# Four tiles of a PEER layer dense: another choice of tiles, and all routing ahead of the dense part

## The chip, the core and the metric

The kernel runs on one core of a Trainium2 chip. The time is device microseconds of one execution; the comparison goes by the median of several. Engines are named as the profile names them: PE (matrix products, with its weight loads as PEld), DVE (vector), ACT (scalar, activation functions), POOL (which issues the gathers of table rows) and SP (which issues all other DMAs). Each engine works through its own instructions in program order and waits where an operand isn't there.

## What is computed

One layer of a decoder trunk, for a prompt of 1024 tokens (tiles 0 to 7 of 128) and a sample group of 32 tokens (the "sample tile", `NT` in the code). Mixers first, then a projection with layer norm, then a PEER layer: each token scores 8 heads of 2 x 128 keys, picks 16 of 128 twice, 16 of the 256 sums, and so 128 experts of 16384; each expert has a row in `peer_u` and one in `peer_v`.

```python
x = layer_norm(ALPHA * x + g1 * mix(x * (1 + sc1) + sh1))
q = einsum('nd,de->ne', h, w_pq); s = einsum('nhpd,hpkd->nhpk', q, peer_keys)
s1, i1 = top_k(s[:, :, 0], 16); s2, i2 = top_k(s[:, :, 1], 16)
top_s, pos = top_k(s1[..., :, None] + s2[..., None, :], 16); idx = i1 * 128 + i2 (at pos)
act  = gelu(einsum('nd,nhkd->nhk', h, peer_u[idx]))
out  = einsum('nhk,nhkd->nd', softmax(top_s) * act, peer_v[idx])
x = layer_norm(ALPHA * x + g2 * out)
```

All inputs and outputs are float32.

## The kernel before

The PEER layer is done in two ways. For the tiles in `GATHERED` POOL gathers the rows that were picked: one gather brings 128 rows of 1024 floats (0.524 MB), one expert for each of 128 tokens. DVE multiplies a row of `peer_u` with the token and sums (L1300, 128 gathers a tile). Then, token by token, the 128 rows of `peer_v` are multiplied with their coefficients on PE (L1357, four instructions' worth for two gathers; a gather of this table is called an item). The sample tile takes 32 + 32 gathers. For the four tiles in `DENSE` the whole tables are streamed through PE: scores of 512 tokens with 128 blocks of 128 experts (`psd`, L1071, 24 matmuls of 512 columns each in three float16 products), GELU (L1161), a product with the gate matrix `G` (L1163), a split into two float16 parts (L1168, L1169), and the second product (`po`, L1178, 256 x 12 matmuls), which is added up in SBUF (L1187). 32 of the 128 score blocks (`PRE`) are done early, in `g_pre`, and parked in DRAM.

`G` comes from `g_weights`: for each dense token a one-hot matrix of the first index and one of the second, scaled by the gate, built by DVE (L1046 to L1049) and, for the last parts of `NL` of 16 tokens, by ACT (L1051); PE multiplies them (L1058), ACT copies PSUM to SBUF in two halves of 64 columns (L1061), and SP stores 32 tokens at a time to `G_d` (L1065).

Before either way, a tile is mixed (`g_mix`: projection with `w_o`, layer norm, transposes) and routed (`g_route`: 16 loads of `w_pq` for each group of tiles, L880, and the top 16 of each list on DVE, L900 to L904; `g_choice` and `g_select`: the second choice). Groups are in `FRONT` ([0, 1], [2, 3], [4, 5], [6]) and `BACK` ([7, NT]).

The order of instructions comes from generators that `run` steps by planned time: each yields estimates for PE, DVE and DMA, `PHASES` scales them by generator and phase, `AHEAD` gives priorities, and `wait` holds a generator until a name is in `ready`. `g_main` holds the dense part back until the gate matrices, the routing of `FRONT` and the early scores are planned; then it opens it (`late`), while `BACK` is mixed and routed beside the first dense steps. `g_gather` plans gathers at all times: rows of the first table of the next tile beside items of the second table of the one before. Both use one ring of six buffers of a row (`rows`, `NROW`). The result of gathered tiles is finished in `finish_tile` or, after the routing, in `g_finish`; dense tiles in `end`.

## Time and profile before

| | us |
|---|---|
| median of 3 runs (3184.49 to 3195.64) | 3193.88 |
| the profiled execution | 3195.18 |
| its span, first to last instruction | 3193.5 |
| mean granted clock of PE, share of full speed | 0.914 |
| PE busy / DVE busy | 2726.1 / 2205.3 |
| DMA moved | 979.03 MB |

The page cuts the span in 40 slices and gives each engine's busy share as a digit; PEclk is the granted clock of PE in tenths, DMA the mean busy share of the 16 DMA engines. A table by stretch gives the busy time of each engine between two times, the number of instructions in brackets, and, last, granted clock, DMA share and GB/s. An engine that is busy all the time bounds its stretch; one that is not may wait for another, and the idle time before its instructions names what ended the wait.

### The profile page before, as it was taken

What the parts mean: (1) busy time and instruction counts of PE and PEld (TensorE: products, weight loads), DVE (VectorE), ACT (ScalarE), POOL (GpSimd) and SP (SyncE); (2) the same over time, 40 slices, a digit from 0 to 9 for tenths busy, and PEclk for the clock granted to TensorE, in tenths of its full rate; (3) what the DMA queues carried; (4) which work ended last, traced back from release to release, by engine and by line L of the source; (5) the groups of instructions that cost most, each with busy time, mean ns of one, the idle gap of its engine ahead of it and who ended that gap; (6) DMA issues with size and microseconds to landing.
All of it is one profiled execution on the core that took longest, in us unless ns stands there. A gap on an engine that the chain in (4) does not pass through costs nothing.

```text
span 3193.5 us, 45027 instructions
## 1 busy us (share of the span) xinstructions
PE 2726.1 (85%) x16366; PEld 1405.0 (44%) x16366; DVE 2205.3 (69%) x5764; ACT 952.3 (30%) x1654; POOL 1312.7 (41%) x1096
## 2 busy tenths in 40 slices
PE   5888995387978699885566999999999999999996
PEld 3447953244546376433322663434444443333331
DVE  2443898867689789767747678848777765655547
ACT  3323234112102145446611223322332322322220
POOL 0000265645444444444434203444555554445443
PEclk7988997688979799997687999999999999999997
DMA  8754798899898899899898647999999999999986
GB/s 294 238 183 146 268 345 291 292 316 320 309 340 311 323 338 347 305 330 359 314 326 313 224 166 244 353 334 336 362 344 361 356 344 328 325 355 342 352 319 212
DMA packets 376498, 979.03 MB, mean 307 GB/s; under 512 B 37477, under 2 KB 116452, under 8 KB 372172
## 3 DMA queue, kind: packets, MB, share of 16 engines
q0 software_dynamic: 156672, 570.49, 49.5%
q1 hardware_dynamic: 219604, 405.67, 36.4%
q8 instruction: 128, 2.10, 0.3%
q14 instruction: 94, 0.77, 0.1%
HBM read 907.07 MB, written 69.02 MB: 306 GB/s over the span
## 4 chain that ended last, share of the span: by engine, by line
PE 49%; DMA 14%; issue 6%; DVE 5%; POOL 3%; ACT 2%; SPq 0%; POOLq 0%; DVEq 0%; ACTq 0%
PE po L1178 16%; PE psd L1071 16%; PE acc L1357 7%; DMA row<-in_peer_v,iT 7%; PE pqr L880 4%; DMA row<-in_peer_u,ii 4%; POOL row L1273 3%; PE py L809 2%; DVE row L1300 1%; DMA G_d<-gs 1%; ACT gs L1061 1%; PE pgm L1058 1%; DMA wo<-in_w_o 1%; PE pvp L279 1%; PE ps L890 1%
## 5 line engine op out<-in xcount | busy, mean ns | idle before, releaser
L1273 POOL DMA_INDIRECT row<-in_peer_u,ii x544 | 666.4, 1225 | 1035.4 <-DVE ii L1296 315.3
L1273 POOL DMA_INDIRECT row<-in_peer_v,iT x544 | 643.0, 1182 | 786.0 <-PE acc L1357 372.9
L1300 DVE SCALAR_TENSOR_TENSOR row<-row,x2u 128x1024 f32<-128x1024 f32 x544 | 660.2, 1217 | 320.7 <-DMA row<-in_peer_u,ii 304.0
L1071 PE MATMUL psd<-xd,us 128*128 128x512 f16 x3072 | 713.6, 383 | 21.4 <-ACT us L1088 14.2
L1178 PE MATMUL po<-vs,coef 128*128 128x512 f16 x3072 | 701.4, 380 | 1.0 <-DVE coef L1169 0.5
L1071 PEld LDWEIGHTS <-us 128*128 128x128 f16 x3072 | 294.6, 99 | 432.1 <-issue 86.7
L1178 PEld LDWEIGHTS <-coef 128*128 128x128 f16 x3072 | 291.6, 98 | 431.8 <-issue 95.4
L1357 PE MATMUL acc<-row,cexp 128*32 128x512 f32 x2176 | 332.6, 654 | 144.7 <-DMA row<-in_peer_v,iT 141.0
L880 PE MATMUL pqr<-x2T,wpq 128*128 128x128 f32 (+1 forms) x2304 | 283.8, 282 | 0.7 <-DVE ns_s L707 0.7
L880 PEld LDWEIGHTS pqr<-x2T,wpq 128*128 128x128 f32 x2304 | 275.6, 198 | 9.9 <-DVE CA L933 1.5
L1161 ACT ACTIVATE act<-psd,scale 128x512 f32<-128x512 f32 x96 | 65.8, 685 | 535.1 <-PE psd L1071 535.0
L1187 DVE SCALAR_TENSOR_TENSOR acc<-po,scale,acc 128x512 f32<-128x512 f32 x248 | 182.8, 744 | 44.7 <-PE po L1178 44.0
L1142 DVE SCALAR_TENSOR_TENSOR vs<-v,vs 128x1024 f16<-128x1024 f32 x128 | 155.9, 1219 | 55.6 <-ACT vs L1141 55.4
L1163 DVE SCALAR_TENSOR_TENSOR act<-act,scale,g 128x512 f32<-128x512 f32 x128 | 95.6, 748 | 140.8 <-ACT act L1161 138.0
L1141 ACT ACTIVATE vs<-v 128x1024 f16<-128x1024 f32 x128 | 134.1, 1054 | 186.0 <-PE po L1178 122.7
L809 PE MATMUL py<-wo,Y 128*128 128x512 f32 (+1 forms) x288 | 141.9, 638 | 32.8 <-DMA wo<-in_w_o 24.0
L1357 PEld LDWEIGHTS acc<-row,cexp 128*32 128x32 f32 x2176 | 48.1, 111 | 269.2 <-DMA row<-in_peer_v,iT 163.4
L1058 PE MATMUL pgm<-ab 128*128 128x128 f16 x1024 | 98.9, 251 | 64.5 <-DVE ab L1048 30.1
L1061 ACT ACTIVATE gs<-pgm 128x256 f32<-128x256 f32 x256 | 125.9, 641 | 49.8 <-PE pgm L1058 33.0
L279 PEld LDWEIGHTS <-w 128*128 128x128 f16 x2160 | 124.2, 100 | 23.7 <-issue 20.6
L1168 ACT ACTIVATE coef<-act 128x512 f16<-128x512 f32 x128 | 80.1, 626 | 153.7 <-DVE act L1163 153.3
L1125 DVE SCALAR_TENSOR_TENSOR us<-u,us 128x1024 f16<-128x1024 f32 x96 | 117.0, 1220 | 11.6 <-ACT us L1124 11.4
(345 smaller groups left out, 2874.2 us busy)
## 6 DMA issues: line engine op xcount, KB each, us to landing
v<-in_peer_v SPq DMA_DIRECT2D x128, 512.0 KB
u<-in_peer_uT SPq DMA_DIRECT2D x96, 512.0 KB
wpq<-in_w_pq SPq DMA_DIRECT2D x80, 512.0 KB
G_d<-gs SPq DMA_DIRECT2D x32, 1024.0 KB
g<-G_d SPq DMA_DIRECT2D x32, 1024.0 KB
wada<-in_w_ada SPq DMA_DIRECT2D x48, 512.0 KB
wf<-in_w_in SPq DMA_DIRECT2D x44, 512.0 KB
wo<-in_w_o SPq DMA_DIRECT2D x40, 512.0 KB
```

The source lines that it names most:

```text
L279: mm(out, lhsT=x if cs is None else y, rhs=y if cs is None else x, start=(i + k == 0), stop=(i == len(ps) - 1 and k == KD - 1))
L809: mm(py[t, e][:ns[t]], lhsT=Y_[t][:, k + j, :ns[t]], rhs=w[:, j, :], start=(k + j == 0), stop=(k + j == KD - 1))
L880: mm(pq[:, i, :ns[t]], lhsT=w[:, k, :], rhs=X2[t][:, k, :ns[t]], start=(k == 0), stop=(k == KD - 1))
L1061: S.activation(gs[e][:, :, t0:t0 + 4].rearrange("p c t -> p t c"), pg[:, :, 64 * e:64 * e + 64], AF.Copy)
L1071: mm(ps, lhsT=us[a][:, k, :], rhs=xd[:, :, b, k, :], start=(m == 0), stop=(m == 23))
L1141: S.activation(vs[:, 0], v, AF.Copy, scale=SV)
L1142: V.scalar_tensor_tensor(out=vs[:, 1], in0=v, scalar=SV, in1=vs[:, 0], op0=ALU.mult, op1=ALU.subtract)
L1178: mm(po, lhsT=d[:, a, i * P:(i + 1) * P], rhs=vs[:, b, c % 2, :], start=(m == 0), stop=(m == 3 * GROUP - 1))
L1187: V.scalar_tensor_tensor(out=a, in0=po, scalar=scale[:, 3:4], in1=a, op0=ALU.mult, op1=ALU.add)
L1273: nc.gpsimd.indirect_dma_start(out=s[:], out_offset=None, in_=A[table], in_offset=bass.IndirectOffsetOnAxis(ap=idx, axis=0))
L1300: V.scalar_tensor_tensor(out=s, in0=s, scalar=1.0, in1=x2, op0=ALU.mult, op1=ALU.mult, accum_out=sv[:, k:k + 1])
L1357: return mm(pv[e][g:g + 32, :], lhsT=l, rhs=s[:, e * 512:e * 512 + 512], start=(j == 0), stop=(j == nj - 1), skip_group_check=True)
```

## The change

- Tiles 3 to 6 are dense instead of 2 to 5; gathered are 0, 1, 2, 7 and the sample tile instead of 0, 1, 6, 7 and the sample tile.
- The groups of mixing and routing become [0, 1], [2, 3], [4, 5], [6, 7, NT], all ahead of the dense part. One PSUM tile takes the scores of up to two tiles and the sample tile, with one copy for all; some sample tiles move into other rings of buffers.
- The dense part waits for one thing more, `ample`: 96 items of the second gathered tile must be planned.
- Items of the third and later gathered tiles have a ring of six rows of their own (`rows2`). To make room, the table `delta` shrinks from 32 x 32 to 8 x 64, a constant of ones is a broadcast, and the x1 rows of the end take over buffers of the dense part.
- `g_gates` gets 5000 of priority and a factor of 0.2 instead of 0.7; its copies take all 128 columns at once, into one buffer that is stored in four parts; `NL` is 3 instead of 6.

```diff
-AHEAD = {"g_mixed": 1000, "g_routed": 1000, "g_even": 1000, "g_odd": 1000}
+AHEAD = {"g_mixed": 1000, "g_routed": 1000, "g_even": 1000, "g_odd": 1000, "g_gates": 5000}
...
-    ("build", {"g_gates": 0.7, "g_even": 0.5, "g_odd": 0.5, "g_mixed": 0.5, "g_routed": 0.5, "g_gather": 0.7}),
-    ("late", {"g_gather": 0.8}),
+    ("build", {"g_gates": 0.2, "g_even": 0.5, "g_odd": 0.5, "g_mixed": 0.5, "g_routed": 0.5, "g_gather": 0.7}),
+    ("dense", {"g_gather": 0.8}),
...
+NROW2 = 6
+AMPLE = 96
...
-GATHERED = (0, 1, 6, 7, NT)
-DENSE = (2, 3, 4, 5)
+GATHERED = (0, 1, 2, 7, NT)
+DENSE = (3, 4, 5, 6)
...
-FRONT = [0, 1], [2, 3], [4, 5], [6]
-BACK = [7, NT],
+GROUPS = [0, 1], [2, 3], [4, 5], [6, 7, NT]
...
-NL = 6
+NL = 3
...
             if b * BB % TB == 0:
-                gs = [sc.tile("gs", [P, 64, TB], F32, 2) for _ in range(2)]
+                gs = sc.tile("gs", [P, P, TB], F32)
...
-                for e in range(2):
-                    S.activation(gs[e][:, :, t0:t0 + 4].rearrange("p c t -> p t c"), pg[:, :, 64 * e:64 * e + 64], AF.Copy)
-                yield 0.6, 1.1, 0.4 * MB
+                S.activation(gs[:, :, t0:t0 + 4].rearrange("p c t -> p t c"), pg, AF.Copy)
+                yield 0.6, 1.1, 0
             if (b + 1) * BB % TB == 0:
-                for e in range(2):
-                    nc.sync.dma_start(G_d[i * (P // TB) + b * BB // TB, :, 64 * e:64 * e + 64, :], gs[e])
+                for e in range(4):
+                    c = slice(32 * e, 32 * e + 32)
+                    nc.sync.dma_start(G_d[i * (P // TB) + b * BB // TB, :, c, :], gs[:, c, :])
...
-                E[i] = cur["fin"].tile(f"e{i}", (P, D))
+                E[i] = sc.tile(f"e{i}", (P, D), F32, 2, "u" if i < 2 else "us")
...
-            if j > len(ops) - 60 and j % 3 == 0:
+            if j >= len(ops) - 8:
                 next(more, None)
...
-    def gather(table, idx):
-        s = cur["rows"].tile("row", (P, D), F32, NROW)
+    def gather(table, idx, own=False):
+        s = cur["rows2" if own else "rows"].tile("row", (P, D), F32, NROW2 if own else NROW)
...
-                    hold[q % 2] = gather("peer_v", iT[:, tok:tok + 1]), hold["c"][:, j % 2, q, :]
+                    hold[q % 2] = gather("peer_v", iT[:, tok:tok + 1], t not in GATHERED[:2]), hold["c"][:, j % 2, q, :]
...
         yield from wait("pre")
+        yield from wait("ample")
         for t in (NT - 1, NT):
             yield from wait(("y", t, 0))
         flush(0)
         cur["build"].close()
         cur["front"].close()
+        ready.add("dense")
         cur["dense"] = Scope("dense")
-        cur["fin"] = Scope("fin")
-        cur["front"] = Scope("late")
-        ready.add("late")
...
-        while "last" not in ready:
-            yield next(dense)
-        flush(0)
-        cur["front"].close()
-        cur["fin"].close()
+        cur["rows2"] = Scope("rows2", "right")
...
+                if done[0] == GATHERED[1] and iv == AMPLE:
+                    ready.add("ample")
```

SP where the dense part starts, before: `G_d<-gs` is the store of the gate matrix, `g<-G_d` its load, `u` a block of the first table, `Y`, `wo` and `keys` belong to the mixing and routing of the last group.

```order
L1065 DMA G_d<-gs 128x2048 x14
L1109 DMA g_13558<-G_d 128x16x128
L1109 DMA g_13607<-G_d 128x16x128
L1117 DMA u<-in_peer_uT 128x1024
L740 DMA g_15345<-ada_d 128x512
L1450 DMA x1f<-x_d 128x512
L800 DMA Y<-ycat_d 128x1024
L800 DMA Y<-ycat_d 128x8x32
L806 DMA wo<-in_w_o 128x2x512 x2
L871 DMA keys<-in_keysT 128x256 x2
```

The same place after: `sd_d<-so` parks the last early scores, the five `r_` rows are the parameters of the finish.

```order
L1090 DMA sd_d<-so 128x512 x3
L1391 DMA r_g_15397<-ada_d 128x1024
L1391 DMA r_ln_g<-in_ln_g 128x1024
L1391 DMA r_ln_b<-in_ln_b 128x1024
L1391 DMA r_ln_g<-in_ln_g 128x1024
L1391 DMA r_ln_b<-in_ln_b 128x1024
L1105 DMA g_15411<-G_d 128x16x128
L1113 DMA u<-in_peer_uT 128x1024 x2
L1131 DMA v<-in_peer_v 128x2x512 x2
L1105 DMA g_15460<-G_d 128x16x128
```

The loads of mixing and routing are gone from between the dense loads, the parameter rows stand there now, and no store of the gate matrix stands directly ahead.

POOL at the end of the program, before: gathers of the first table (`peer_u`) and of the second (`peer_v`).

```order
L1273 DMA row<-in_peer_u,ii 128x1024
L1273 DMA row<-in_peer_v,iT 128x1024 x3
L1273 DMA row<-in_peer_u,ii 128x1024
L1273 DMA row<-in_peer_v,iT 128x1024 x3
L1273 DMA row<-in_peer_u,ii 128x1024
L1273 DMA row<-in_peer_v,iT 128x1024 x71
```

And after:

```order
L1270 DMA row<-in_peer_u,ii 128x1024
L1270 DMA row<-in_peer_v,iT 128x1024
L1270 DMA row<-in_peer_u,ii 128x1024
L1270 DMA row<-in_peer_v,iT 128x1024 x2
L1270 DMA row<-in_peer_u,ii 128x1024
L1270 DMA row<-in_peer_v,iT 128x1024 x128
```

The first table's rows end 128 items before the end instead of 71.

DVE at the very end, before: `row<-pfold` is the sum of the sample tile's items, the last thing that was gathered.

```order
L786 SCALAR_TENSOR_TENSOR row<-row,mv,r_ln_b 128x1024
L1420 TENSOR_TENSOR row<-pfold,g2s 32x512 x2
L1425 TENSOR_TENSOR row<-row,x1f 32x1024
L781 BN_STATS st<-row 32x6 x2
L782 BN_AGGR mv<-st 32x2
L354 TENSOR_SCALAR ve<-mv 32x1
L785 SCALAR_TENSOR_TENSOR row<-row,mv,r_ln_g 32x1024
```

And after, where `acc` is the sum of a dense tile:

```order
L361 TENSOR_TENSOR mv<-vy,vy_25416 128x1
L360 TENSOR_SCALAR vy_25472<-vy_25472 128x1
L786 SCALAR_TENSOR_TENSOR acc_15409<-acc_15409,mv,r_ln_b 128x1024
L361 TENSOR_TENSOR mv<-vy,vy_25472 128x1
L786 SCALAR_TENSOR_TENSOR acc_15410<-acc_15410,mv,r_ln_b 128x1024
```

The program ended with the sample tile's gathered sum, and ends with two dense tiles now.

## Rows read from the trace of the kernel before

**Rows 1.** The page: span, DMA totals, one costly group (busy, mean ns of one).

```profile
span 3193.5 us, 45027 instructions
...
DMA packets 376498, 979.03 MB, mean 307 GB/s; under 512 B 37477, under 2 KB 116452, under 8 KB 372172
...
L1300 DVE SCALAR_TENSOR_TENSOR row<-row,x2u 128x1024 f32<-128x1024 f32 x544 | 660.2, 1217 | 320.7 <-DMA row<-in_peer_u,ii 304.0
```

**Rows 2.** Busy time by stretch: PE, PEld, DVE, ACT, POOL; clock, DMA share, GB/s.

```profile
0.00:350.00 350.00, 275.21 (x2186) 180.10 (x2187) 138.46 (x534) 110.71 (x209) 3.31 (x8) 0.88 0.62 208
350.00:1000.00 650.00, 498.93 (x3437) 325.67 (x3437) 529.65 (x1794) 148.89 (x282) 343.82 (x285) 0.84 0.91 322
1000.00:1210.00 210.00, 168.07 (x1174) 112.03 (x1173) 171.73 (x702) 58.96 (x124) 93.52 (x75) 0.89 0.89 317
1210.00:1300.00 90.00, 88.69 (x670) 57.02 (x671) 79.84 (x386) 47.72 (x96) 37.46 (x25) 1.00 0.88 331
1300.00:1602.00 302.00, 202.95 (x1410) 111.01 (x1402) 218.84 (x339) 172.41 (x391) 140.13 (x108) 0.82 0.91 333
1602.00:2000.00 398.00, 341.17 (x1739) 172.27 (x1739) 274.51 (x824) 94.82 (x155) 115.18 (x96) 0.92 0.75 254
...
2250.00:2600.00 350.00, 348.29 (x1708) 144.33 (x1707) 269.24 (x386) 103.81 (x129) 192.77 (x152) 1.00 0.98 355
...
2000.00:3150.00 1150.00, 1137.23 (x5709) 445.33 (x5707) 764.69 (x1093) 318.19 (x400) 568.53 (x490) 1.00 0.95 340
```

**Rows 3.** PE: the chain; L1071, L1178, L1357 in 2000:3150; a gather in 2250:2600.

```profile
1904.42 5.18 PE psd L1071 x24
...
2000.00:3150.00 1150.00, 422.83 (x1848) 176.17 (x1848) 1.00 0.95 340
2000.00:3150.00 1150.00, 584.37 (x2567) 243.34 (x2567) 1.00 0.95 340
2000.00:3150.00 1150.00, 176.10 (x1288) 25.77 (x1286) 1.00 0.95 340
...
L1273 POOL DMA_INDIRECT row<-in_peer_u,ii x89 | 110.1, 1237 | 64.8 <-DVE row L1300 35.7 <-issue 18.9 <-PE acc L1357 5.6
```

**Rows 4.** In 1602:2000: PE on L880, on L809; DVE on tiles TV, WK.

```profile
1602.00:2000.00 398.00, 61.20 (x512) 0.92 0.75 254
1602.00:2000.00 398.00, 33.81 (x64) 0.92 0.75 254
1602.00:2000.00 398.00, 41.97 (x284) 0.92 0.75 254
1602.00:2000.00 398.00, 18.04 (x40) 0.92 0.75 254
```

**Rows 5.** Groups in 1300:1602: busy us, mean ns, idle before and its releasers.

```profile
L1061 ACT ACTIVATE gs<-pgm 128x256 f32<-128x256 f32 x202 | 96.8, 642 | 44.1 <-PE pgm L1058 32.0 <-DMA G_d<-gs 11.9
L1273 POOL DMA_INDIRECT row<-in_peer_u,ii x62 | 83.1, 1341 | 86.1 <-DVE row L1300 39.6 <-PE acc L1357 33.8 <-issue 8.8
L1051 ACT ACTIVATE ab<-ab,fl 128x128 f16<-128x128 f16 x144 | 44.4, 392 | 40.4 <-DVE ab L1048 40.4
L1049 DVE TENSOR_TENSOR ab<-ab,fx 128x1280 f16<-128x1280 f16 x24 | 19.6, 820 | 0.1
```

**Rows 6.** The timeline at the first GELU of the dense part.

```profile
1602.13 0.69 ACT L1161 ACTIVATE act<-psd,scale 128x512 f32<-128x512 f32 x1 [3.55 <-PE psd L1071]
```

**Rows 7.** The timeline at the end of the dense part.

```profile
3142.71 3.41 PE L1178 MATMUL po<-vs,coef 128*128 128x512 f16 x15
...
3153.17 12.51 SPq L1204 DMA_DIRECT2D out_y_p<-acc  x4
```

**Rows 8.** DMA issues: count, KB each, median us to landing.

```profile
u<-in_peer_uT SPq DMA_DIRECT2D x96, 512.0 KB
...
g<-G_d SPq DMA_DIRECT2D x32, 1024.0 KB
...
row<-in_peer_u,ii POOLq DMA_INDIRECT x544, 7.5
```

More of the change, by code (lines that the diff above doesn't have):

```diff
@@ L112, in run @@
         now = 0.0
-        late = False
+        dense = False
         while parts:
-            if "late" in ready and not late:
-                late = True
+            if "dense" in ready and not dense:
+                dense = True
                 now = max(busy)
@@ L287, in load_consts @@
             C[nm] = load(nm, A[nm])
-        ones = C["ones"] = work("ones4", [4, P])
-        V.memset(ones, 1.0)
         o1 = C["ones1"] = work("ones1", [P, 1])
         V.memset(o1, 1.0)
+        C["ones"] = o1[0:4].to_broadcast([4, P])
         V.memset(Cst, 0.0)
@@ L798, in g_mix @@
             if t > 0:
-                Y_[t] = slab("Y", (P, KD, P))
+                Y_[t] = half("Y", (P, KD, NS)) if t == NT else slab("Y", (P, KD, P))
                 nc.sync.dma_start(Y_[t][:, :, :ns[t]], ycat_d[t, :, :, :ns[t]])
@@ L813, in g_mix @@
                 if t not in z:
-                    z[t] = slab("z")
+                    z[t] = (xslab if t == NT else slab)("z")
                 if t == ts[0] or t == NT:
@@ L853, in g_mix @@
             if t == NT:
-                x2T = X2[t] = slab("x2T", (P, KD, P))
+                x2T = X2[t] = half("x2T", (P, KD, NS))
                 for e in range(2):
@@ L866, in g_route @@
         m = len(ts)
+        nq = sum(ns.values())
         for t in ts:
-            top[t] = (work("TV", [P, 16, 16], F32, BUFS["t"]), work("TI", [P, 16, 16], U16, BUFS["t"]), keep("rt", [P, 2, 8, 16], bufs=6))
+            top[t] = (work("TV", [P, 16, 16], F32, BUFS["t"]), work("TI", [P, 16, 16], U16, BUFS["t"]), keep("rt", [P, 2, 8, 16], bufs=7))
         for h in range(8):
@@ L876, in g_route @@
                 nc.sync.dma_start(w, A["w_pq"][c])
-                pq = bank("pqr", (P, 2, P))
+                pq = bank("pqr", (P, 2 * P + NS))
                 for i, t in enumerate(ts):
                     for k in range(KD):
-                        mm(pq[:, i, :ns[t]], lhsT=w[:, k, :], rhs=X2[t][:, k, :ns[t]], start=(k == 0), stop=(k == KD - 1))
-                qc = work("qc", (P, 2, P), F32, 2)
+                        mm(pq[:, i * P:i * P + ns[t]], lhsT=w[:, k, :], rhs=X2[t][:, k, :ns[t]], start=(k == 0),
+                           stop=(k == KD - 1))
+                qc = work("qc", (P, 2 * P + NS), F32, 2)
+                S.activation(qc[:, :nq], pq[:, :nq], AF.Copy)
                 for i, t in enumerate(ts):
-                    if i and ns[t] == P:
-                        continue
-                    j = i + 1
-                    while j < m and ns[ts[j]] == ns[t]:
-                        j += 1
-                    S.activation(qc[:, i:j, :ns[t]], pq[:, i:j, :ns[t]], AF.Copy)
-                for i, t in enumerate(ts):
-                    mm(sb[i // 2][:ns[t], i % 2, p, :], lhsT=qc[:, i, :ns[t]], rhs=kt[:, p, :], start=True, stop=True)
+                    mm(sb[i // 2][:ns[t], i % 2, p, :], lhsT=qc[:, i * P:i * P + ns[t]], rhs=kt[:, p, :], start=True, stop=True)
                 yield 1.95 * m, 0, 0.58 * MB
@@ L1191, in ready_end @@
             for i, t in enumerate(DENSE):
-                E[i] = cur["fin"].tile(f"e{i}", (P, D))
+                E[i] = sc.tile(f"e{i}", (P, D), F32, 2, "u" if i < 2 else "us")
                 nc.sync.dma_start(E[i], x1_d[t])
-                yield
+            yield
             for i in range(len(DENSE)):
@@ L1264 @@
     V.tensor_copy(iota16, it32)
-    delta = keep("delta", [P, 32, 32], BF16)
+    delta = keep("delta", [P, 8, 64], BF16)
     nc.gpsimd.memset(delta, 0.0)
-    nc.gpsimd.affine_select(out=delta, in_=delta, pattern=[[1, 32], [-1, 32]], compare_op=ALU.not_equal, fill=1.0, base=0,
+    nc.gpsimd.affine_select(out=delta, in_=delta, pattern=[[1, 8], [-1, 64]], compare_op=ALU.not_equal, fill=1.0, base=32,
                             channel_multiplier=0)
     coef = {}
-    def gather(table, idx):
-        s = cur["rows"].tile("row", (P, D), F32, NROW)
+    def gather(table, idx, own=False):
+        s = cur["rows2" if own else "rows"].tile("row", (P, D), F32, NROW2 if own else NROW)
         nc.gpsimd.indirect_dma_start(out=s[:], out_offset=None, in_=A[table],
@@ L1308, in finish @@
             if smp:
-                s2 = keep("s2", [NS, P])
+                s2 = keep("cT_", [P, P], bufs=2)[:NS]
                 for q in range(4):
@@ L1543, in g_mixed @@
         before = None
-        for ts in FRONT:
+        for ts in GROUPS:
             if before:
@@ L1549, in g_mixed @@
             before = ts
-        yield from wait("late")
-        for ts in BACK:
-            yield from g_mix(ts)
-            ready.add(("mixed", ts[0]))
-            yield from wait(("routed", ts[-1]))
     def g_routed():
-        for ts in FRONT + BACK:
+        for ts in GROUPS:
             yield from wait(("mixed", ts[0]))
@@ L1562, in g_chosen @@
     def g_chosen():
-        for ts in list(FRONT) + list(BACK):
+        for ts in GROUPS:
             yield from wait(("scored", ts[0]))
             yield from g_choice(ts, early=(ts[0] == 0))
-            if ts == FRONT[-1]:
-                ready.add("chosen")
-        ready.add("last")
+        ready.add("chosen")
     pend = []
@@ L1632 @@
     run(g_main(), g_even(), g_odd(), g_gates(), g_pre(), g_cond(), g_mixed(), g_routed(), g_chosen(), g_gather())
-    for nm in ("fin", "dense", "xd", "rows"):
+    for nm in ("fin", "dense", "rows2", "xd", "rows"):
         cur[nm].close()
```

7 lines of the change are left out of this document (2 added, 5 removed).

## Prediction

> **What bounds the kernel now.** I read the page first [rows 1], then one table of busy times by stretch [rows 2], then the stretches on either side of the place where the dense part starts. The reader should see two halves with different limits. From 2000 us to 3150 us PE is busy 1137.2 of 1150 us at a granted clock of 1.00, the 2.4 GHz level, while DMA runs at 340 GB/s [rows 2]: PE sets the time there. From 350 us to 1602 us no engine is full: the four stretches give PE 958.6, DVE 1000.0 and DMA 0.88 to 0.91 of 1252 us [rows 2]. DMA is the nearest to full, and it moves 322, 317, 331 and 333 GB/s. From 1602 us, where the first GELU of the dense part starts [rows 6], to 2000 us nothing is full: PE 341 of 398 us, DMA 0.75, 254 GB/s, because tiles 7 and the sample tile are mixed and routed beside the first dense steps. So a change is worth what it does to three numbers: the time T1 at which the dense part starts, the time T2 from there to the last gathered row, and what remains after it.
>
> **What is moved across T1.** Counted in the two programs' orders: before, the first accumulation of the second dense product on PE stands behind 174 items of the second table, and the first dense coefficient on DVE behind 319 rows of the first table. After, these are 218 and 380. The wait for 96 items of the second gathered tile does that; it is a wait of the plan, and on the chip it shows as items standing ahead on PE's queue, with every dense matmul behind them. So 44 + 61 = 105 gathers of 0.524 MB, 55.1 MB, come ahead of the dense part. The mixing of tile 7 and the sample tile adds its loads and stores, four transfers of 0.52 MB and four of a quarter of that, 2.6 MB. The group of three tiles costs no further w_pq or w_o in the first half, since [6] had loaded them already; the second half loses 16 w_pq and 8 w_o of 128 x 1024 floats, 0.524 MB each, 12.6 MB in all. Total bytes go from 979.0 [rows 1] to 966.4 MB.
>
> **T1.** By 1602 us the old kernel has moved 0.35·208 + 0.65·322 + 0.21·317 + 0.09·331 + 0.302·333 = 479.1 MB (thousands of us times GB/s) [rows 2]. The new one needs 479.1 + 57.7 = 536.8 MB. At the 333 GB/s of the last stretch the 57.7 MB take 173 us: T1 = 1775. At 355, the rate of 2250 to 2600 [rows 2], they take 163. The engines must also carry what comes with it. PE: 61.2 us of key scores and 33.8 of the output product, read where they stand today [rows 4], and 44 items of 0.573 us, 120 us; PE idles 142 us from 1000 to 1602 alone [rows 2], so this is covered. DVE: 61 rows of 1.217 us [rows 1], 74 us; routing of two tiles, 42.0 for the lists and 18.0 for the second choice [rows 4]; layer norm and small steps, an estimate of 25 from some twenty 1024-wide steps at that same 1.217; and NL 6 to 3, which widens 32 instructions from 10 to 13 tokens, 0.3·0.820·32 = 8 us [rows 5]. That is 167 us in 173. DVE is busy 299 of the 392 us from 1210 to 1602 [rows 2]; it would have to be busy 466 of 565, or 0.82.
>
> The gate steps themselves get lighter for ACT. 96 scalings of 0.392 us leave it, 38 us. 256 copies of 0.642 us [rows 5] become 128 of twice the width; one costs between 0.642, if the width were free, and 2·0.642. I take the upper end, so that nothing is gained: 0.642 for 256 elements is about as much for each as 0.392 for the 128 of a scaling. That is 0 to 82 us of ACT's time, and ACT is busy 172 of 302 us there, hence off the path either way. The single output buffer must wait for four stores where a half waited for one; today such waits cost ACT 11.9 us in 302 [rows 5]. With 16 blocks it is some 20 us of ACT, covered by the same idle time. What is queued behind it on ACT is the splitting of u for the early scores, which PE has slack for.
>
> The Trainium skill (SBUF — State Buffer, section SBUF: two separate sides) says that a DVE instruction in a two-port mode locks GpSimd out of a shared port, so that gather descriptors can't be written meanwhile. That speaks against moving work from ACT to DVE. Here one gather instruction took 1341 ns in the gate stretch and 1237 in 2250 to 2600 [rows 3, 5], and POOL idles over half of the time there: by the rule the 8 us of DVE would hold POOL up for at most 8 us and the sum would be 3192; by the rows it stays 3184.
>
> **T2, T3, T4.** One matmul of 512 columns takes 5.18/24 = 0.2158 us [rows 3]. Between 2000 and 3150 us PE ran 1848 + 2567 of them, 952.8 us, and 1288/4 = 322 items [rows 3]; (1137.2 - 952.8)/322 = 0.573 us each. In the new order the last item stands with 552 score and 828 output matmuls still behind it, so **T3** = 1380·0.2158 = 298 us of pure dense work, bound by PE. Before it stand 3972 matmuls and 326 items: 857 + 187 = 1044 us of PE. DMA must move in that stretch 966.4 - 536.8 - 43 = 386.6 MB, where 43 is what T3 loads and stores (23 u and 33 v of 0.524, 7 g of 1.05 [rows 8], 6 for x1, results and parked scores). At 355 GB/s that is 1089 us, at the 340 of the old second half 1137. So the gathered stretch changes its bound, from PE to DMA. I take **T2** = 1089, because the 355 stretch had DMA at 0.98 and is the one nearest to a DMA limit; bounds 1044 and 1137. The own ring of six rows for the second table lets more gathers wait at once, but they share the same DMA engines: it is worth nothing where DMA is full, and keeps it full. At T1 five parameter rows of 0.5 MB go ahead of the first g and u on SP's queue, 3.6 MB, some 10 us at 355, in which PE has only gathered items: DMA stays busy, so T2 by bytes holds it. **T4**, from the last matmul to the end, is 22 us: the old dense part ends its matmuls at 3146 and issues its last store by 3166 [rows 7], plus an estimate of 2 for landing. The loads of x1 now come 8 steps before the end instead of 60; they have some 8 us, about the 7.5 us landing of a row [rows 8], so 0 to 8 us more, and I take 0. The old tail of gathered items after that point, 3146 to 3193, goes.
>
> **Sum.** 1775 + 1089 + 298 + 22 = 3184 us of span, against 3193.5. The profiled execution took 1.7 more than its span and lies 1.3 above the median of 3193.88, so the forecast is 3184 + 0.4 = **3184**. Compared with today, what follows the first GELU shrinks from 1591 to 1409 us, and the first GELU comes 173 later: a near break-even with a small gain. The smaller one-hot table, the removed constant and the shared buffers are worth nothing: some memory and one memset.
>
> The Trainium skill (HBM Reference, section Specifications (TRN2)) gives about 425 GB/s for a core that streams alone. By it T2 would fall to PE's 1044 and the sum to about 3139; the row says 355 GB/s at a share of 0.98, and I go by the row.
>
> **Rivals.** *The first half soaks it up.* The idle tenth of DMA before 1602 us is not DMA's doing: rows wait for DVE and PE [rows 5]. With routing early and gates ahead, the stretch from 1000 us may run at 355: (536.8 - 282.1)/0.355 = 717, T1 = 1717, total 3126. For it: PE and DVE have idle time. Against: more work per us is asked of both.
>
> *Slower: DVE becomes the bound of the first half.* Routing, gates and row products now stand in one queue of DVE. From 1210 us it has 79.8 + 218.8 + 167 = 466 us to do. It decides once DVE can't be kept above 0.82 busy. At the 0.725 of 1300 to 1602 [rows 2] that takes 642 us, T1 = 1852, total 3261; at 0.78 it is 597, total 3216. For it: 0.725 is what that mix of waits gives today. Against: 0.89 from 1210 to 1300 [rows 2].
>
> *The change doesn't do what it says:* PE stays the bound of the gathered stretch, T2 = 1044. That is inside the sum's bounds, total 3139, and counts with the first rival.
>
> **How the numbers follow.** 0.46 for the sum, 3150 to 3215 with T2 from 1065 to 1110 and T1 from 1765 to 1790; 0.27 for the soaked first half; 0.27 for DVE. The range leaves out 2 in 10 and runs from 3115 to 3250. Within 0.5% is 3178 to 3210, about what a measurement can tell from no change. Of the sum's 0.46 some 0.18 lies below that, 0.25 in it and 0.03 above. Faster 0.45, within 0.26, slower 0.29.
>
> **What would show it.** Right: first GELU near 1775 us, the stretch before it at 330 GB/s or more with DVE at 0.8 or over; then DMA at 0.97 and PE a few per cent idle, waiting for rows of the second table, until about 2860; then some 300 us of PE alone with DMA under half. Wrong: a first GELU after 1820 with DVE idle between waits, or before 1730; PE full through the gathered stretch; or a last stretch in which PE waits for u or v.

## The result: 3286.55 us, slower, and all of the miss lies ahead of the dense part

The changed kernel takes 3286.55 us (median of 4 runs, 3272.81 to 3302.27) against 3193.80: a ratio of 1.0298, 95% interval 1.0241 to 1.0355. The forecast was 3184, with a range of 3115 to 3250. The profiled execution took 3295.28 us.

The page of the changed kernel (span, DMA totals, and two groups, answering [rows 1] and the copies of [rows 5]):

```profile
span 3293.2 us, 44626 instructions
...
DMA packets 375182, 964.84 MB, mean 293 GB/s; under 512 B 37445, under 2 KB 115396, under 8 KB 374956
...
L1056 ACT ACTIVATE gs<-pgm 128x512 f32<-128x512 f32 x128 | 124.4, 1083 | 129.7 <-PE pgm L1054 74.9
```

Its first GELU, from the timeline of ACT:

```profile
1880.69 0.69 ACT L1157 ACTIVATE act<-psd,scale 128x512 f32<-128x512 f32 x1 [2.86 <-PE psd L1067]
```

One reading of the prediction is off: the row at 1602.13 in [rows 6] is the second GELU of the kernel before. Its first starts at 1596.95:

```profile
1596.95 0.69 ACT L1161 ACTIVATE act<-psd,scale 128x512 f32<-128x512 f32 x1 [3.66 <-PE psd L1071]
```

So T1, the start of the first GELU of the dense part, went from 1597 to 1881, by 284 us instead of 173.

The stretches of the changed kernel, as in [rows 2] (PE, PEld, DVE, ACT, POOL; granted clock, DMA share, GB/s):

```profile
1000.00:1240.00 240.00, 169.87 (x1029) 90.80 (x1028) 164.81 (x653) 39.46 (x75) 109.48 (x100) 0.82 0.87 311
1240.00:1870.00 630.00, 434.00 (x3096) 267.98 (x3095) 495.52 (x1525) 225.63 (x339) 312.88 (x215) 0.85 0.84 299
1870.00:2660.00 790.00, 768.92 (x3810) 306.15 (x3811) 559.43 (x817) 221.53 (x284) 432.31 (x360) 0.99 0.99 362
2660.00:2966.00 306.00, 291.54 (x1507) 101.88 (x1505) 138.17 (x188) 73.86 (x95) 133.53 (x126) 0.96 0.91 321
2966.00:3270.00 304.00, 301.73 (x1384) 135.43 (x1382) 179.94 (x230) 92.42 (x115) 0.00 (x0) 0.99 0.38 120
3270.00:3293.00 23.00, 0.00 (x0) 0.00 (x0) 19.18 (x74) 0.00 (x0) 0.00 (x0) 0.51 0.23 91
```

Behind T1 the table reads much as forecast: DMA at 0.99 up to 2660 us and 0.91 from there to the last item, with PE close behind it (0.97 and 0.95 busy); then 304 us of PE alone, then 23 us. Ahead of it nothing is full: from 1240 to 1870 us DMA has 0.84 and moves 299 GB/s where 333 was assumed, DVE is busy 0.79 and PE 0.69 of the time. Who waits for whom there (engine, tile and line that waits, what it waits for; us in total, times, longest):

```profile
POOL row L1270 <- DVE row L1297: 121.1, 42, 8.9
...
PE acc L1354 <- DMA row<-in_peer_v,iT: 106.0, 17, 12.8
ACT ab L1047 <- DVE ab L1044: 92.8, 17, 18.9
POOL row L1270 <- PE acc L1354: 88.3, 30, 7.5
ACT so L1089 <- PE psd L1067: 76.0, 22, 9.5
ACT gs L1056 <- PE pgm L1054: 70.7, 26, 14.8
DVE row L1297 <- DMA row<-in_peer_u,ii: 68.8, 36, 5.6
...
ACT gs L1056 <- DMA G_d<-gs: 20.2, 6, 7.5
```

Every engine waits for another: POOL for free buffers, PE and DVE for the rows that POOL issued late, ACT for PE and DVE. No one of them is the bound.

### The profile page after: what moved, and what is told of

Same layout as the page of the kernel before. It is cut to its first block, busy times and chain, and to the rows that moved or that the text cites. A ratio compares the mean times of both kernels' runs of the same rounds, so it can differ in the third digit from the quotient of the medians.

```text
span 3293.2 us, 44626 instructions
## 1 busy us (share of the span) xinstructions
PE 2731.8 (83%) x16366; PEld 1401.7 (43%) x16366; DVE 2216.0 (67%) x5763; ACT 909.6 (28%) x1394; POOL 1339.3 (41%) x1096
## 5 line engine op out<-in xcount | busy, mean ns | idle before, releaser
L1270 POOL DMA_INDIRECT row<-in_peer_u,ii x544 | 697.1, 1281 | 908.1 <-DVE ii L1293 311.8
L1067 PE MATMUL psd<-xd,us 128*128 128x512 f16 x3072 | 723.0, 386 | 47.1 <-ACT us L1120 21.8
L1354 PE MATMUL acc<-row,cexp 128*32 128x512 f32 x2176 | 337.7, 672 | 218.8 <-DMA row<-in_peer_v,iT 218.1
L881 PE MATMUL pqr<-x2T,wpq 128*128 128x128 f32 (+1 forms) x2304 | 290.6, 286 | 5.9 <-ACT gs L1056 5.4
L1354 PEld LDWEIGHTS acc<-row,cexp 128*32 128x32 f32 x2176 | 48.4, 112 | 359.5 <-DMA row<-in_peer_v,iT 247.9
L1056 ACT ACTIVATE gs<-pgm 128x512 f32<-128x512 f32 x128 | 124.4, 1083 | 129.7 <-PE pgm L1054 74.9
L809 PE MATMUL py<-wo,Y 128*128 128x512 f32 (+1 forms) x288 | 137.7, 626 | 14.7 <-DMA Y<-ycat_d 14.3
L1054 PE MATMUL pgm<-ab 128*128 128x128 f16 x1024 | 82.3, 232 | 36.5 <-DVE ab L1044 9.7
```

Of the source, the lines that this page charges most:

```text
L809: mm(py[t, e][:ns[t]], lhsT=Y_[t][:, k + j, :ns[t]], rhs=w[:, j, :], start=(k + j == 0), stop=(k + j == KD - 1))
L881: mm(pq[:, i * P:i * P + ns[t]], lhsT=w[:, k, :], rhs=X2[t][:, k, :ns[t]], start=(k == 0), stop=(k == KD - 1))
L1056: S.activation(gs[:, :, t0:t0 + 4].rearrange("p c t -> p t c"), pg, AF.Copy)
L1067: mm(ps, lhsT=us[a][:, k, :], rhs=xd[:, :, b, k, :], start=(m == 0), stop=(m == 23))
L1270: nc.gpsimd.indirect_dma_start(out=s[:], out_offset=None, in_=A[table], in_offset=bass.IndirectOffsetOnAxis(ap=idx, axis=0))
L1354: return mm(pv[e][g:g + 32, :], lhsT=l, rhs=s[:, e * 512:e * 512 + 512], start=(j == 0), stop=(j == nj - 1), skip_group_check=True)
```

## The experiments

Of each run: gathers issued before T1, T1, the rest of the span behind T1, and the span, all of the profiled execution. The ratio to the kernel before, with its interval, is there where several executions were timed. The others are single executions, good to some 15 us: the changed kernel's own four spread over 30.

| run | gathers | T1 | behind | span | ratio |
|---|---|---|---|---|---|
| before | 492 | 1597 | 1597 | 3193.5 | 1 |
| changed | 602 | 1881 | 1413 | 3293.2 | 1.0298 (1.0241 to 1.0355) |
| e1 no wait for 96 | 592 | 1851 | 1518 | 3368.5 | |
| e2 old gate steps | 613 | 1864 | 1409 | 3272.7 | |
| e10 old plan of gates | 631 | 1884 | 1392 | 3276.3 | |
| e3 rows later | 602 | 1856 | 1411 | 3266.3 | |
| a2 the same, timed | 601 | 1864 | 1413 | 3277.8 | 1.0245 (1.0214 to 1.0276) |
| e5 seven buffers | 626 | 1847 | 1399 | 3245.7 | |
| e6 five buffers | 568 | 1902 | 1487 | 3388.9 | |
| e8 one ring | 602 | 1871 | 1443 | 3314.3 | |
| e9 narrow products | 529 | 1668 | 1514 | 3182.0 | |
| a1 items first | 622 | 1878 | 1383 | 3260.7 | 1.0232 (1.0197 to 1.0267) |
| e12 combined | 651 | 1835 | 1477 | 3311.9 | 1.0426 (1.0400 to 1.0451) |
| c1 rows held from 64 | 504 | 1767 | 1437 | 3204.5 | 1.0068 (1.0038 to 1.0097) |
| c2 rows held from 32 | 448 | 1746 | 1455 | 3200.3 | 1.0019 (0.9995 to 1.0042) |
| e4 before, new gates | 467 | 1580 | 1672 | 3252.2 | |
| e7 before, new tiles | 511 | 1635 | 1598 | 3233.8 | |
| e11 before, seven buffers | 521 | 1611 | 1611 | 3222.1 | 1.0115 (1.0093 to 1.0137) |
| b1 before, items first | 500 | 1598 | 1590 | 3188.5 | 1.0047 (1.0024 to 1.0070) |
| b2 before, seven, items first | 524 | 1641 | 1569 | 3209.3 | 1.0083 (1.0055 to 1.0112) |

**The wait for 96 items.** The prediction held it to be what makes the dense part late.

```diff
         yield from wait("pre")
-        yield from wait("ample")
```

> The changed kernel without its wait for 96 items of the second gathered tile. In the program's order 214 items and 375 rows of the first table still stand ahead of the dense part (218 and 380 with the wait), but no dense matmul is left behind the last item (1380 with it). If the wait is what made the dense part late, the first GELU falls from 1881 us to well under 1850. If the stretch before it is late for reasons of its own, the first GELU stays within 15 us of 1875, and only the end changes: 5352 dense matmuls of 0.2158 us and 330 items of 0.573 us are 1344 us of PE, so the span is about 1875 + 1344 + 22 = 3241 us, against 3293 with the wait.

T1 came 30 us earlier with 10 gathers fewer, of the 284 us by which it had grown; neither expectation's number came. So the wait is not what makes the dense part late, and 589 of the 598 gathers stand ahead of it without the wait too; the prediction was wrong there. But the span grew by 75 us, 127 over the 3241 expected. POOL's timeline shows the gathers stop for 246 us behind the start:

```profile
1912.91 1.75 POOL L1270 DMA_INDIRECT row<-in_peer_v,iT  x1 [0.30 <-issue]
2160.83 0.94 POOL L1270 DMA_INDIRECT row<-in_peer_v,iT  x1 [246.17 <-PE acc L1354]
```

PE is full all that time, so the stop alone loses nothing. What is lost is PE's: behind T1 the item matmuls keep it busy for 313.0 us (1328 records) instead of 184.1 (1312). The busy time of L1354, e1 first, then the changed kernel:

```profile
1851.00:3368.00 1517.00, 313.02 (x1328) 0.99 0.80 281
```

```profile
1881.00:3293.00 1412.00, 184.09 (x1312) 0.98 0.83 296
```

That is 129 us, and the split items below are the reason: in e1 163 pairs of records stand alone between dense matmuls behind T1, in the changed kernel two.

**The gate steps**, in both kernels.

```diff
-AHEAD = {..., "g_gates": 5000}
+AHEAD = {...}
-    ("build", {"g_gates": 0.2, ...
+    ("build", {"g_gates": 0.7, ...
-NL = 3
+NL = 6
-                gs = sc.tile("gs", [P, P, TB], F32)
+                gs = [sc.tile("gs", [P, 64, TB], F32, 2) for _ in range(2)]
```

> The changed kernel with the gate steps of the kernel before: no priority, factor 0.7, copies in two halves with two buffers each, NL 6. 230 items and 384 rows stand ahead of the dense part, 16 gathers or 8.4 MB more than in the changed kernel. Theory of the gate steps (put ahead on every engine, they hold up the rows and items, so that DMA falls to 299 GB/s): the rate goes back to 333 GB/s, first GELU near 1800 us, span near 3190. Theory of the mix (routing of three tiles and the gate steps share DVE with the row products, whatever the order of the gate steps): first GELU near 1905, span within 15 us of 3293.

> The changed kernel with the old plan of the gate steps (no priority, factor 0.7), but with their new form (one copy, one buffer, NL 3). 246 items and 384 rows stand ahead of the dense part. If the place of the gate steps is what slows the gathers, the pace from 1000 us on is 2.68 us, as with the old gate steps altogether, and the first GELU comes near 1905 for 28 gathers more than with them... less what the shorter end gives back: span near 3285. If the form (a single buffer stored in four parts) slows them, the pace stays at 2.81 and the span is over 3310.

> The kernel before with the new gate steps alone: priority 5000, factor 0.2, one copy of all columns, one buffer stored in four parts, NL 3. 160 items and 303 rows stand ahead of the dense part, 30 gathers or 15.7 MB fewer than before. Theory of the gate steps: the stretch from 1210 us on runs at 299 GB/s instead of 332, 114.7 MB take 384 us, first GELU near 1594 in spite of the 30 gathers less; the span some 30 us over 3193, since 30 more gathers come behind it. Theory of the mix: 332 GB/s as before, first GELU near 1555, span within 15 us of 3193.

In the changed kernel they are worth little: T1 17 us earlier with 11 gathers more, the span within the spread; old plan with new form (e10) gives the same span, so the form costs nothing that shows. From 1000 us to T1 a gather leaves every 2.68 us in e2 and 2.60 in e10, against 2.80 in the changed kernel: it is the place of the gate steps that slows the gathers. But more gathers stand ahead, and T1 hardly gains; neither theory's T1 came in e2. In the kernel before the new gate steps cost 59 us in a single execution, but behind T1: 25 gathers fewer stand ahead of it, and POOL issues 78 gathers behind the last dense matmul instead of 12.

**The switch.** SP at the start of the dense part of the changed kernel; the two loads of u occupy its queue for 18.87 us:

```profile
1842.87 0.32 SPq L1391 DMA_DIRECT2D r_g<-ada_d  x1
...
1845.77 0.49 SPq L1105 DMA_DIRECT2D g<-G_d  x1
1846.31 18.87 SPq L1113 DMA_DIRECT2D u<-in_peer_uT  x2
```

```diff
+        for _ in range(4):
+            yield next(dense)
         load_rows()
         yield from dense
```

> The changed kernel with the loads of the five parameter rows behind the first four dense steps instead of ahead of them. Same counts ahead of the dense part. Theory of the switch (the 35 us in which PE has almost nothing between the last early score and the first dense one are lost for good): first GELU near 1855, span near 3265. Theory of the bytes (DMA is full at 361 GB/s in those 41 us, so nothing is lost there): first GELU 10 to 25 us earlier, span within 10 us of 3293.

> The changed kernel with the parameter rows behind the first four dense steps, a second time, with an interval. Theory of the switch: 3265 within 8 us again, 0.993 of the changed kernel's 3286.6. Theory of the bytes (DMA was full in the 41 us of the switch, so they come back later): the first look was at the fast end of the spread, and the median is 3278 or more.

T1 came 17 to 25 us earlier. The median is 3265.5, 21 us under the changed kernel's; but the ratios' intervals overlap (1.0214 to 1.0276 and 1.0241 to 1.0355), so a gain for good is likely and not proved.

**The tiles alone, in the kernel before** (3 to 6 dense, 0, 1, 2, 7 gathered, routing of [7, NT] still beside the dense part).

> The kernel before with the other choice of tiles alone: 3 to 6 dense, and 0, 1, 2, 7 and the sample tile gathered; groups, gate steps and rings as before. 182 items and 331 rows stand ahead of the dense part, 20 more than before. At a pace of 2.9 us a gather the first GELU comes near 1660 instead of 1602; by bytes (10.5 MB at 333 GB/s) near 1634. The span stays within 30 us of 3193 by either theory, as the gathers only change sides.

T1 is 38 us later for 19 gathers, 2 us each, as by bytes. The execution took 3235.6 us and one of the kernel before beside it 3209.1; that kernel's executions lie between 3168 and 3209, so 26 us are just about what chance can make, and the span says little.

**The ring.** `NROW` 7 with `NROW2` 5, `NROW` 5, and all rows in the first ring.

> The changed kernel with seven buffers of a row instead of six in the first ring, and five instead of six in the own ring; one buffer less in two rings of small tiles makes the room. 620 gathers stand ahead of the dense part (598 before). Theory of the ring: from 1000 us to the first GELU one gather leaves every 2.81 us, because a row's buffer is held for about six times that, while DMA, DVE and PE all have time left. With seven buffers it is 6/7 of it, 2.40 us: 332 gathers from 1000 us on take 798, first GELU near 1800 us (1690 if the stretch from 350 to 1000 us gains as well), span near 3190. Theory of the mix (DVE and PE are late with other work, and a further buffer only waits longer): 2.8 us for each gather, first GELU at 1900 or later, span 3280 or more.

> The changed kernel with five buffers in the first ring. 566 gathers stand ahead of the dense part. Theory of the ring: 6/5 of 2.81 us, 3.37 us for a gather from 1000 us on; at the pace of 2.26 us up to 1000 us first GELU near 1937, at 6/5 of that too near 2100. Theory of the mix: unchanged pace, first GELU near 1790 with the 32 gathers that are fewer.

> The changed kernel without the own ring: all rows go through the six buffers of the first ring. Same counts ahead of the dense part, so the first GELU stays within 15 us of 1881 by all theories. Behind it 490 gathers are left. If the ring sets the pace there too, it is the 2.4 us of the kernel before from 2000 to 2600 us: 1176 us instead of 1085, span near 3384. If DMA sets it, 355 GB/s are reached with six buffers as with twelve and the span stays within 20 us of 3293.

One gather left every 3.09, 2.80 and 2.58 us from 1000 us to T1 with five, six and seven buffers: the ring matters, with about half of the weight that its theory gave it. With seven buffers a row of the second table is also held longer, 20.0 us on average from its gather to its last matmul (from 1240 us to T1) against 17.9. T1 moved by 21 and 34 us only. The own ring is worth 30 us behind T1 (1443 against 1413): DMA has 0.96 and 347 GB/s without it from 1870 to 2400 us, 0.98 and 357 with it.

**DVE's work.** The row products over 64 of 1024 columns (out, in and the token's row all cut to `[:, 0:64]`).

> The changed kernel with row products of the first table over 64 of the 1024 columns, so its output is not the layer's. The gathers and their bytes stay; each product takes DVE some 0.15 us instead of 1.22. 525 gathers stand ahead of the dense part (598 before), since the planner sees the shorter product. Theory that DVE's work sets the first half (busy 0.83 from 1240 to 1780 us): about 1.07 us of DVE less for each of some 160 rows from 1000 us on; the pace falls from 2.81 us a gather towards the 1.9 to 2.0 that full DMA allows, first GELU near 1500. Theory of the ring: a row is held some 2 of 17 us less, 2.5 us a gather, first GELU near 1630. Theory of latency elsewhere (PE's items): pace unchanged at 2.8, first GELU near 1700.

The pace stayed at 2.75 us a gather, so DVE's work is not what sets it. Yet T1 fell to 1668, with 73 gathers fewer ahead and 380 us of DVE's work less (944 against 1324): the routing got done sooner, and PE's last key score ends at 1437 us instead of 1612. The run changes two things at once, DVE's work and, through the planner, the number of gathers ahead. The stretch up to T1, e9 first, then the changed kernel:

```profile
0.00:1668.00 1668.00, 1324.96 (x9575) 852.76 (x9576) 943.82 (x4370) 529.12 (x907) 583.88 (x537) 0.88 0.85 304
```

```profile
0.00:1881.00 1881.00, 1377.91 (x9695) 861.48 (x9696) 1324.13 (x4460) 527.59 (x906) 773.51 (x610) 0.84 0.83 290
```

**Items first, and split items.** The matmuls of the second table's rows get a priority of 20000 instead of 2000.

```diff
-AHEAD_S, AHEAD_U, AHEAD_V, AHEAD_F = 2000, 2000, 2000, 4000
+AHEAD_S, AHEAD_U, AHEAD_V, AHEAD_F = 2000, 2000, 20000, 4000
```

> The changed kernel with a priority of 20000 instead of 2000 for the matmuls of the second table's rows. 616 gathers stand ahead of the dense part (598 before). Theory that rows wait for their turn on PE: they are held less than the 16 to 18 us of the changed kernel, the pace from 1000 us on falls from 2.81 to about 2.6 us a gather, first GELU near 1855 in spite of 18 gathers more, span near 3255. Theory that they wait for their landing and for the pair's other row: pace unchanged, first GELU near 1920, span within 15 us of 3287.

The pace is 2.65 us, between the two, but rows of the second table are held as long from their gather to their last matmul (17.8 us from 1240 us to T1, 17.9 in the changed kernel): they don't wait for PE's turn. The span gained comes behind T1 (1383 against 1413). What holds the row was not settled further.

> The changed kernel with the old gate steps, seven buffers in the first ring and five in the own one, the parameter rows behind the first four dense steps, and a factor of 1.1 instead of 0.8 for the gathers beside the dense part, so that 996 instead of 1380 dense matmuls are left behind the last item. Sum of the single steps: first GELU 17 us earlier by the gate steps, 15 by the parameter rows, 34 by the ring, but 260 items ahead, so near 1880; behind it 284 items, PE's floor 5352 x 0.2158 + 284 x 0.573 = 1318 us and 22: span near 3220. If DMA idles in the first half for another reason, it is 3270 as the old gate steps alone.

The span came out 92 us over the sum of the single gains. T1 was early, 1835 instead of 1880; behind it 1477 us passed instead of 1340. PE shows the larger part of these 137 us: its items took 241.3 us instead of 288 x 0.573 = 165. The rest was not taken apart; PE idles for 59 us behind T1. The timeline of PE in the combined kernel:

```profile
2726.99 1.05 PE L1354 MATMUL acc<-row,cexp 128*32 128x512 f32 x2
2727.97 0.39 PE L1067 MATMUL psd<-xd,us 128*128 128x512 f16 x1
2728.29 1.04 PE L1354 MATMUL acc<-row,cexp 128*32 128x512 f32 x2
2729.26 0.39 PE L1067 MATMUL psd<-xd,us 128*128 128x512 f16 x1
```

And in the changed kernel:

```profile
2706.66 1.06 PE L1354 MATMUL acc<-row,cexp 128*32 128x512 f32 x8
2707.65 3.41 PE L1174 MATMUL po<-vs,coef 128*128 128x512 f16 x15
```

The eight records of two items take 1.06 us together; two of them alone take 1.05. The planner lays single instructions of items between dense ones: 106 such pairs of records stand behind T1 in the combined kernel. Behind T1 that makes 241.3 us for 288 items in the combined kernel (0.84 each), 266.2 for 362 in e11 (0.74), 313.0 for 332 in e1 (0.94), and 184.1 for 328 in the changed one (0.56).

> The kernel before with seven buffers of a row instead of six, the smaller one-hot table of the changed kernel, and one buffer less in two rings of small tiles for the room. 518 gathers stand ahead of the dense part (493 before). If the ring limits the first half as it did in the changed kernel (2.81 to 2.58 us a gather from 1000 us on), the first GELU comes at about 1595 with 25 gathers more ahead, and the span is 40 to 60 us shorter, near 3145. If DMA or DVE limits it in the kernel before, the first GELU comes near 1660 and the span stays within 15 us of 3193.

> The kernel before with that priority alone. In its order 16 matmuls of items stand singly between dense ones, now none; 500 gathers ahead of the dense part instead of 493. Price of a single one by the traces: 1.04 us, against 1.07 for four together, so 0.77 us each. Theory of the split items: 16 x 0.77 = 12 us less, span near 3173. Theory of the turn on PE: the first half gains too, span near 3160. Neither: 3185 within 10 us.

> The kernel before with seven buffers of a row and that priority. With seven buffers alone 84 matmuls of items stood singly between dense ones, now none; 521 gathers ahead as there, and 863 dense matmuls are left behind the last item instead of 53. Theory of the split items: 84 x 0.77 = 65 us less than the 3222.6 with seven buffers alone, so near 3158 and faster than the kernel before. Theory that the time between 1800 and 2200 us is lost because POOL's gathers stop there for the routing, whatever PE's order: 3205 or more.

With priority the price in b2 is 196.3 us for 360 items, 0.55 each: 70 us less than in e11, about the 65 expected. The busy time of L1357 behind T1, e11 first, then b2:

```profile
1611.00:3222.00 1611.00, 266.22 (x1448) 0.97 0.85 300
```

```profile
1641.00:3209.00 1568.00, 196.31 (x1440) 0.97 0.86 307
```

Of that, 42 us show behind T1 (1569 against 1611), but T1 itself came 30 us later. So the price of a split is shown, and a gain for the whole kernel is not: b1 (3202.8 us, above all three numbers expected) and b2 (3211.9, the number of the other theory, which was not followed further) are slower than the kernel before by less than 1%, clear of noise.

**Gathers held back**, the routing and gates as in the changed kernel. From row 64 (or 32) of tile 2's first table the gathers wait for the dense part; items first and rows later are in it as well.

```diff
-        yield from wait("ample")
...
+            late = us and t == GATHERED[2] and iu >= 64 and "dense" not in ready
+            if late and not vs:
+                yield from wait("dense")
+                continue
-            if us and need in ready and (not vs or ...
+            if us and not late and need in ready and (not vs or ...
...
+                if t == GATHERED[2] and 64 <= iu < 64 + 8 and "dense0" in held:
+                    def f(f=f):
+                        with tc.issue_after(held["dense0"]):
+                            f()
```

> The changed kernel, in which the rows of the first table of the third gathered tile are held back, from the 64th on, until the dense part has started; the wait for 96 items goes, the parameter rows come later and items have priority as in a2 and a1. All routing and gates stay ahead. 500 gathers stand ahead of the dense part instead of 598, and 333 dense matmuls behind the last item instead of 1380. Theory of the pace: 102 gathers at 2.4 to 2.5 us less, first GELU near 1630; behind it 468 MB at 355 GB/s, 1319 us, then 72 and 22: span near 3045. Theory of the chain of routing and gates: first GELU at 1850 or later; behind it PE's floor of 1375 us: 3230 or more.

> The same, held back from the 32nd row on. 444 gathers stand ahead of the dense part, no dense matmul behind the last item. Theory of the pace: first GELU near 1490, behind it 506 MB at 355 GB/s, 1425 us, and 30: span near 2950. If routing and gates on PE and DVE become the limit on the way, the first GELU stays near that of the run with 64 and the span comes out some 60 us over it, since more gathers follow. Theory of the chain: 3230 or more.

The theories of the pace and of the chain both missed. T1 is 1767 and 1746: not 1630 and 1490, and not 1850. What the expectation of c2 said for routing and gates as the limit came true for T1, which stayed near c1's; the span did not come out 60 us over it, but 4 under. In c2 POOL issues nothing from 1383 us on, for 358 us, held by the order until the dense part begins, and the dense part hardly comes sooner for it. The two stretches in c2:

```profile
1400.00:1600.00 200.00, 174.41 (x1374) 127.27 (x1374) 143.97 (x551) 104.45 (x159) 0.00 (x0) 0.97 0.42 152
1600.00:1800.00 200.00, 139.17 (x766) 66.33 (x764) 136.90 (x312) 79.95 (x109) 21.45 (x16) 0.86 0.58 205
```

And its waits from 1400 to 1745 us:

```profile
POOL row L1271 <- DVE row L1298: 358.3, 1, 358.3
DVE us L1085 <- ACT us L1084: 53.5, 12, 8.8
ACT so L1089 <- PE psd L1067: 32.3, 13, 5.4
ACT ab L1047 <- DVE ab L1044: 31.1, 15, 9.8
...
ACT gs L1056 <- PE pgm L1054: 29.2, 12, 4.5
...
ACT gs L1056 <- DMA G_d<-gs: 23.5, 7, 4.8
PE pgm L1054 <- DVE ab L1044: 20.7, 3, 11.5
```

What is left is routing, gate steps and early scores, each step of which goes from PE to ACT to DVE and back; no engine is full (PE, the busiest, has 0.87 from 1400 to 1600 us), and yet it takes until 1746. In this order, that is a floor under T1 which the forecast didn't have: c2 has 44 gathers fewer ahead than the kernel before, and starts the dense part 149 us later. Above the floor, 97 gathers (601 in a2, which loads the parameter rows as late as c1 does, against 504) cost 97 us, 1.0 each, and the step from 448 to 504 only 21. Of the kernels that compute the whole layer none beats the kernel before; c2 comes level with it (0.9995 to 1.0042) and is 2.7% under the changed kernel, by T1 alone: what follows it is 42 us longer.

## Why the prediction was wrong, step by step

- **T1, wrong by 106 us: 1775 forecast, 1881 measured.** The bytes were right (0.290 x 1881 = 546 MB by T1, 537 forecast) and so was DVE's work (1324 us, 1306 forecast). The rate was wrong: 299 GB/s from 1240 to 1870 us. The step that failed is "at the 333 GB/s of the last stretch", with its companion "so this is covered": what lies on PE and DVE was taken as hidden beside DMA, and so the routing of tile 7 and the sample tile was charged with its 2.6 MB alone, 8 us. What came is the sign that the prediction itself had named as wrong: a first GELU after 1820 us, with DVE idle between waits.
- **What it costs by the runs.** From the kernel before to e7, the tiles: T1 + 38 with 19 gathers. From e7 to c1, with about as many gathers (511, 504) but the routing moved ahead: + 132. From c1 to a2, 97 gathers: + 97. From a2 to the changed kernel, the parameter rows ahead of the first loads: + 17 (25 by e3). So the 116 gathers cost 135 us where 105 were given 165; the rows cost 17 where DMA was to hide them; and the rest cost 132 instead of 8. The charge that was too high for the gathers hid some 30 us of the error. c1 holds the new gate steps too; by e2 and e4 (17 us with 11 gathers more; 17 earlier with 25 fewer, at 1.0 us a gather) they are an estimated 8 to 28 of the 132. The routing has an estimated 105 to 125. This is argued from differences of single traces, and c1 differs from both neighbours in more than one step (items first, no wait for 96); the routing was not measured by itself.
- **Where it lies in the traces.** PE's last key score ahead of T1 ends at 1293 us in the kernel before, 1311 in e7, 1586 in c1 and 1612 in the changed kernel; gate steps and 16 to 18 of the 32 early scores follow it. The new gate steps go ahead of the routing, so the cleaner pair is e7 and e2, both with the old ones: 1311 and 1503, 192 us later. Yet T1 is 1864 in e2, hardly under the changed kernel's: routing and gate steps count together, and not which of them goes first. Not tested: tile 6 routed by itself and tile 7 and the sample tile behind it, still ahead of the dense part. As it is, the gates of the dense tile 6 come behind the routing of a group of three tiles.
- **A better reading was there.** DVE's busy share up to the start of the dense part is 1138.5 of 1602 us in the kernel before, 0.71, and 0.70 in e7, c1 and the changed kernel. With the forecast's own 1306 us of DVE's work that is 1837, still 44 us short of what came. It is no law (0.57 in e9, 0.69 in c2), but where no engine is full, work moved ahead lengthens the stretch at about the shares that it has.
- **The rival "DVE becomes the bound" came nearest** with T1 = 1852 and 3261, and got its sign right; its mechanism did not hold. From 1210 us to T1 DVE had 514.7 us to do, not 466, because it had fallen behind before (0.69 busy from 1000 to 1240), and it was busy 0.77. But e9, with some 300 us less of DVE's work than c1 (944 against 1245), has a T1 that is some 140 us under what c1's, 1.0 us for each of 25 further gathers and the 17 us of the parameter rows would give: an estimate of 0.5 us for each us of DVE, where a bound would give a whole one. That its number came near was in part luck.
- **The wait for 96 items as the cause of the later start: wrong** (e1). It keeps the order behind T1 sound, and is worth its place.
- **T2, T3, T4 were right.** The last item ends at 2965, so T2 is 1084 (1089 forecast; 362 GB/s up to 2660 us, 355 assumed); the last matmul ends at 3268, so T3 is 303 (298) and T4 25 (22). The price of an item is 184.1/328 = 0.561 us (0.573). The gathered stretch is bound by DMA, as forecast, by a small margin: PE is busy 0.97 of it, and T2 is 40 us over PE's 1044 by the rival in which PE stays the bound. By the page of the Trainium skill that was weighed (HBM Reference, section Specifications (TRN2)) T2 would have been that 1044, and the row decided.
- **The small terms.** The bytes up to 1602 us add up to 479.0 MB, not 479.1, which changes nothing. G's store waits cost ACT 20.2 us (20). The copies were bounded between 0.642 and 1.284 and taken at the upper end: one took 1.083, in sum 124.4 us of busy time against 125.9 of the page before, so nothing was gained, as taken. The switch was given "some 10 us" with DMA busy. DMA was busy (361 GB/s from 1840 to 1881 us), but PE was not: SP's first u landed 26 us after the rows were issued and PE had a gap of 35 (last early score 1837.3, first dense one 1872.7).

## What to carry to other kernels

Where no engine is full, a stretch is a chain of hand-offs: price work that is moved into it at the shares that the stretch has now, and not at the peak of its busiest resource. Here the one came 44 us short, the other 106. Before moving independent work ahead of a critical start, ask what the start waits for without it: 97 gathers before the start (c1 and a2) cost 97 us there and gave back 24 behind it. Count how an order splits groups of instructions that run side by side: four that share PE cost as much as one.

## What was not expected of the hardware

- Matmuls of 32 columns on PE: two records alone 1.05 us, eight together 1.06. The Trainium skill (TensorE: Matmul & The Clock Gate, section Why this matters for your kernels) says that small-M matmuls in distinct column groups run concurrently, 2.38 times as fast with three tiles. The trace agrees in kind; the loss when dense matmuls come between them is shown by the rows alone.
- A gather instruction takes POOL longer in the stretch of the gate steps: 1.09 us on average from 1000 to 1240 us in the changed kernel (109.48 us for 100), 1.41 from 1240 to 1667 us. In the same stretch of e9, where DVE is busy 0.63 of the time instead of 0.84, it is 1.28. The stretch lies ahead of T1 in both; the changed kernel first, then e9:

```profile
1240.00:1667.00 427.00, 329.80 (x2478) 222.35 (x2477) 360.57 (x1197) 168.69 (x258) 198.59 (x141) 0.90 0.85 300
```

```profile
1240.00:1667.00 427.00, 324.89 (x2327) 191.72 (x2325) 267.71 (x1010) 174.55 (x255) 202.99 (x159) 0.88 0.93 337
```

  So in this pair a busier DVE goes with slower gather instructions, by 0.13 us. By the Trainium skill (SBUF — State Buffer, section SBUF: two separate sides) a DVE instruction in a two-port mode and an instruction of GpSimd lock a shared pair of ports against each other. That this is the reason here is not shown. DVE's share alone does not set it, for from 1000 to 1240 us it is 0.69. For the 215 gathers from 1240 to 1870 us it would be an estimated 28 us of POOL's time, where the prediction allowed 8. As the pace of the gathers is nearly the same in both runs (2.80 and 2.75 us), it was not what set T1.
